# Output token sums behind the state updates, a head's squares as one step, operand loads of the output block behind P7

## The chip, the cores and the metric

The kernel runs on one core of one Trainium2 chip. The metric is device time in microseconds (us). Before the change, three runs took 1650.22, 1650.51 and 1651.77 us, so the median is 1650.51 us. One more execution was recorded by the hardware profiler. It took 1648.75 us by itself, and its instructions span 1647.0 us; TensorE ran at a mean granted clock of 0.998 of full speed.

## What is computed

Two layers act on one sequence of 512 tokens with 2048 features. In each layer:

- RMSNorm of the input, then one projection `z = h @ w_in` whose columns are split among a gated linear attention (4 heads: q, k of 128 columns, v of 256) and a softmax attention (8 heads of 128 columns), each with a SiLU gate of its own.
- Linear attention, in chunks of 64 tokens: `S_c = diag(a_c) S_{c-1} + sum_s k_dec_s v_s^T`, and each token reads the state of its own chunk, `o = q S_c`.
- Softmax attention: each token sees its own chunk of 64 and the eight before it (with 512 tokens: all earlier chunks), with a learned bias by clipped distance.
- Each head's output is RMS-normalised (`o * rsqrt(mean(o^2) + eps)`), scaled and multiplied by its SiLU gate. The two groups are concatenated, projected by `w_out`, normalised again and added to the layer's input.

Everything is in float32.

## The kernel before

**Products.** Float32 accuracy is made of two reduced parts: an operand is split into a high part (a cast on ScalarE, `split` at L108, or `high` at L203 for weights) and a low part (the difference, on VectorE, L109 and L207). Three matmuls, high x high, low x high and high x low, make one product. `std_gemm` (L323) multiplies in the plain way. `fast_gemm` (L399 and L409) multiplies two 512-column weight blocks at once by a scheme with seven sub-products (P1 to P7) instead of eight. For these, sums of token blocks (S1 to S4) and sums of weight blocks are needed. The token sums of a layer's input and of its output are formed by `make_sums` (L613 to L622: four adds on VectorE for each of four column blocks c; `put` then splits each result and stores it to DRAM, L607). Later a job loads them back into a ring of four buffers `sa` (L187).

**Jobs.** A `fast_gemm` is 28 jobs: (P1, c) for c = 0 to 3, four of P5, eight of P6 and P3 mixed, then four each of P7, P2 and P4. A job is 12 matmuls over 512 columns. Its weight load (`fetch`, L154) is traced up to five jobs ahead, its cast and its low part three to four ahead. In one layer the order is: the attention gates, the linear attention's gates, av, two attention query/key products (feature-major), the linear attention's key/query product (`PAIRS[4]`), its value product (`PAIRS[5]`), the output projection's first two blocks (plain), and the last two blocks as a `fast_gemm` with `end=True`.

**Work beside the products.** The attention heads and the linear attention are written as generators, put on a list `tasks`. After every job `pump` advances the first task by some steps (`rate`, 2.1 or 2 steps a job). `until` pumps at once until a condition holds. `delayed` runs a function after so many more steps. `attend` runs a pair of heads a and b by the list `ORDER`: S (scores of a 128-token tile, L847 to L857), T (transposes of its probabilities, L869 to L874), P (`mix`, L886: probabilities times values, into 128 columns of one PSUM bank `ps_o` a head, and a square sum of that tile on ScalarE, L892), G (`gate`: VectorE adds at L896, a power on GpSimd at L447, four multiplies at L900). Eight steps after G comes `turn`: transposes (L911), scaling (L914) and split, the store of the head's output for the output sums (L917, `fa`) and, for the second head of a pair, the store of the pair's two operand halves to DRAM (L923, `oa`). The pairs come in the order 2/3, 0/1, 6/7, 4/5.

**Loads of the operands.** `fetch_operands` runs after each job of the value product. Once (P1, 3) is past, it loads each pair's first half (L1176) into the buffer that P1's operand has left, as soon as the code has traced that pair's `turn`. The second halves are loaded at P4 (L1180).

**Linear attention.** For each of eight units (head h, half p): `outer` (L1048), `states` (L1067 and L1069, four chained updates on VectorE), `read` (L1082), `norm` (squares at L1092, L451, power on GpSimd), `gate` (L1100) and `turn` (L1110, L1121). `early_sums` forms the output sums of column blocks 2 and 3 beside the last four units, one of its steps for three of theirs. The sums of blocks 0 and 1 come after all units.

**What sets the order.** The code's order of tracing is a priority. A planner with a cost model of its own then puts each engine's instructions in order. Where an instruction isn't ready by that model, a later one goes first. On the chip each engine, and SyncE's and GpSimd's DMA queues too, works strictly through its planned order. `tc.issue_after(x)` adds that what is traced inside it stands behind x on x's engine. Buffers of one tag are shared: 8 of `t2` (most intermediate rows), 4 PSUM banks `mm` and 4 `ax`.

Of the kernel before, what the change touches and what calls it, by code (L numbers as in the profile page):

```python
# [15 lines left out]
P = 128  # L16
# [18 lines left out]
def hybrid_trunk(  # L35
# [107 lines left out]
    last_cast, last_load, last_low, last_norm = [None], [None], [None], [None]  # L143
    made = set()
    lows = []
    rows = {}
# [451 lines left out]
    def make_sums(l, end, tags, parts, chunks=range(4)):  # L598
        stage = [0]
        dst = (so_d if end else sa_d)[l]  # L600

        def put(name, c, src):
            op = slot(tags[stage[0] % 4], [2, 512], F32R)
            stage[0] += 1
            with tc.issue_after(last_cast[0]):
                split(op[:, 0, :], op[:, 1, :], src)
            nc.gpsimd.dma_start(dst[name, c], flat(op))  # L607
            made.add((l, end, name, c))

        for c in chunks:  # L610
            a11, a12, a21, a22 = parts(c)
            yield
            nc.vector.tensor_tensor(out=a22, in0=a21, in1=a22, op=ALU.subtract)  # L613
            put("S1", c, a22)
            yield
            nc.vector.tensor_tensor(out=a21, in0=a11, in1=a21, op=ALU.subtract)
            put("S3", c, a21)
            yield
            nc.vector.tensor_tensor(out=a22, in0=a22, in1=a11, op=ALU.subtract)
            put("S2", c, a22)  # L620
            yield
            nc.vector.tensor_tensor(out=a12, in0=a12, in1=a22, op=ALU.add)  # L622
            put("S4", c, a12)
            yield

# [57 lines left out]
    def layer(l):  # L683
# [150 lines left out]
        class Head:  # L834
# [41 lines left out]
            def mix(self, i):  # L876
                hd = self.hd
                if self.ps_o is None:
                    self.ps_o = aux()
                    self.sg = sgt([4, P])  # L880
                    nc.sync.dma_start(
                        self.sg, sg_d[l][1][:, hd * P : (hd + 1) * P].rearrange("(t p) c -> p t c", p=P)
                    )
                o = self.ps_o[:, i * P : (i + 1) * P]
                for j in range(i + 1):
                    nc.tensor.matmul(  # L886
                        o, self.pt[i][:, j * P : (j + 1) * P],
                        av[hd // 4, j // 2][:, j % 2, (hd % 4) * P : (hd % 4 + 1) * P],
                        start=(j == 0), stop=(j == i),
                    )  # L890
                jk = t2((P,), BF16)
                nc.scalar.activation(jk, o, AF.Square, scale=P ** -0.5, accum_out=self.ss[:, i : i + 1])  # L892

            def gate(self):
                v, cf = sm(4), sm(4)
# [9 lines left out]
            def turn(self):  # L905
                c, kk = self.hd // 2, self.hd % 2
                if kk == 0:
                    turned[c] = [slot(tag, [2, 512], F32R) for tag in ("g16", "g17")]
                ps = aux()
                for t in range(NT):  # L910
                    nc.tensor.transpose(ps[:, t * P : (t + 1) * P], self.sg[:, t, :], ident)  # L911
                kt = 8 + self.hd
                f = t2()
                nc.scalar.activation(  # L914
                    f, ps, AF.Copy, scale=gcol[:, l * 2 * KT + KT + kt : l * 2 * KT + KT + kt + 1]
                )
                nc.gpsimd.dma_start(of_att[l][c][:, kk, :], f)  # L917
                ks = slice(kk * 256, (kk + 1) * 256)
                for half in range(2):
                    z = turned[c][half]  # L920
                    split(z[:, 0, ks], z[:, 1, ks], f[:, half * 256 : (half + 1) * 256])
                    if kk:
                        nc.gpsimd.dma_start(oa_d[l][half, c], flat(z))  # L923

        ORDER = (
            "aS3 aS2 aS1 aS0 aT3 bS3 aT2 aP3 bS2 aT1 aP2 bS1 aT0 aP1 bS0 aP0 - aG "
            "bT3 bT2 bP3 bT1 bP2 bT0 bP1 bP0 - bG"
        ).split()

        def attend(hd, qk):  # L930
            heads = {"a": Head(hd, qk, 0), "b": Head(hd + 1, qk, 1)}

            def turn(h):
                h.turn()
                if h.hd % 2:
                    heads_done.add(hd)

            for _ in range(5 if hd == HEADS[0] else 0):
                yield
            for step in ORDER:  # L940
                if step == "-":
                    yield
                    continue
                h = heads[step[0]]
                if step[1] == "S":
                    h.scores(int(step[2]))
                elif step[1] == "T":
                    h.trans(int(step[2]))
                elif step[1] == "P":
                    h.mix(int(step[2]))  # L950
                else:
                    h.gate()
                    delayed.append([8, lambda h=h: turn(h)])
                yield
# [73 lines left out]
        class Unit:  # L1028
# [24 lines left out]
            def states(self):  # L1053
                h, p = self.h, self.p
                tag = "sg" if (2 * h + p) % 2 else "bias"
                self.sg = tmp.tile([P, 2, 256], F32, tag=tag, name=nm(tag), bufs=2)
                nc.sync.dma_start(
                    self.sg,
                    sg_d[l][0][p * 256 : (p + 1) * 256, h * 256 : (h + 1) * 256].rearrange("(t p) c -> p t c", p=P),
                )  # L1060
                prev = self.prev
                for q in range(4):
                    n = 4 * p + q
                    cur = self.st[:, q, :]
                    u = self.ps_u[q % 2][:, (q // 2) * 256 : (q // 2 + 1) * 256]
                    if prev is None:
                        nc.vector.tensor_copy(cur, u)  # L1067
                    else:
                        nc.vector.scalar_tensor_tensor(  # L1069
                            out=cur, in0=prev, scalar=a_end[:, h * 8 + n : h * 8 + n + 1], in1=u,  # L1070
                            op0=ALU.mult, op1=ALU.add,
                        )
                    prev = cur

            def read(self):
# [95 lines left out]
        def fetch_operands(k, c):  # L1171
            passed.add((k, c))
            for i in range(4):
                if ("P1", 3) in passed and 2 * i in heads_done and (0, i) not in op_att:
                    op_att[0, i] = slot(f"a11{i}", [2, 512], F32R)
                    nc.sync.dma_start(flat(op_att[0, i]), oa_d[l][0, i])  # L1176
# [193 lines left out]
```

## Time and profile before

| what | value |
|---|---|
| median of three runs | 1650.51 us (1650.22 to 1651.77) |
| profiled execution | 1648.75 us |
| its span, first to last instruction | 1647.0 us |
| TensorE matmul busy | 1626.9 us |
| VectorE busy | 1226.5 us |
| ScalarE busy | 904.6 us |
| GpSimd busy | 164.3 us |
| moved by DMA | 470.64 MB, mean 286 GB/s |

PE is TensorE's matmul, PEld its weight load, DVE VectorE, ACT ScalarE, POOL GpSimd, SP SyncE. In a timeline a row has the start and the length in us, the engine, the line of the kernel, the operation, the tile written and the tiles read, the shape and a count; in brackets the idle time before it and what ended it. A matmul record lasts longer than its turn on the engine, because matmuls are pipelined: their starts are about 0.23 us apart for 512 columns. A row of SPq or POOL with DMA_DIRECT2D is the issue of a transfer, not the transfer. In the table of waits a row names the waiting engine and line, then what it waited for, the total in us, the number of times and the longest.

### The profile page before, as it was taken

The numbers are of one execution on the slowest core, as the hardware profiler recorded it, in microseconds if no ns is written. First come the engines' busy times: TensorE is split into PE (matmuls) and PEld (weight loads), VectorE is DVE, ScalarE is ACT, GpSimd is POOL, SyncE is SP. The second block draws the span as 40 slices with busy tenths as digits, with TensorE's granted clock in tenths as the row PEclk, the third lists the DMA queues.
The fourth block names the chain that finished last, engine by engine and source line by source line (L and its number), as shares of the span: only waits on it lengthen the run. The fifth ranks groups of instructions, "written<-read, shape, count | busy, mean of one in ns | idle before, by whom it ended". The sixth has DMA issues, their size and how long they took to land.

```text
span 1647.0 us, 24886 instructions
## 1 busy us (share of the span) xinstructions
PE 1626.9 (99%) x9030; PEld 1393.8 (85%) x9030; DVE 1226.5 (74%) x1579; ACT 904.6 (55%) x1515; POOL 164.3 (10%) x261
## 2 busy tenths in 40 slices
PE   9999999999999999999999999999999999999997
PEld 7888889999988877688888888899999888776886
DVE  7567776877877875778877676768777768757887
ACT  7444544566666644454784445445657665445553
POOL 1210000000000101310132000000001001013101
PEclk9999999999999999999999999999999999999999
DMA  9978896858858796899879797868587678878996
GB/s 378 344 276 315 284 316 223 309 183 303 281 187 291 249 352 202 285 378 332 294 257 379 270 331 268 319 222 304 193 308 263 204 265 281 321 226 299 363 345 230
DMA packets 150778, 470.64 MB, mean 286 GB/s; under 512 B 16428, under 2 KB 35636, under 8 KB 150656
## 3 DMA queue, kind: packets, MB, share of 16 engines
q1 hardware_dynamic: 127632, 389.36, 68.4%
q0 software_dynamic: 22304, 78.41, 12.2%
q8 instruction: 71, 1.16, 0.3%
q10 hardware_dynamic: 720, 1.28, 0.2%
q14 instruction: 51, 0.42, 0.1%
HBM read 396.88 MB, written 72.11 MB: 285 GB/s over the span
## 4 chain that ended last, share of the span: by engine, by line
PE 98%; ACT 1%; DMA 1%; DVE 0%; issue 0%; DVEq 0%; POOL 0%; SPq 0%; ACTq 0%; POOLq 0%
PE mm L409 45%; PE mm L323 22%; PE mm L399 20%; PE ax L886 2%; PE ax L409 1%; PE ax L1048 1%; PE ax L869 1%; PE ax L1082 1%; PE ax L717 1%; PE ax L847 1%; PE ax L849 1%; PE ax L848 1%; DMA sa<-S 0%; PE ax L911 0%; PE ax L551 0%; PE ax L748 0%
## 5 line engine op out<-in xcount | busy, mean ns | idle before, releaser
L409 PE MATMUL mm<-wh,sa 128*128 128x512 f32 x1536 | 486.1, 391 | 2.4 <-DMA sa<-S 1.3
L203 ACT CAST wh<-raw 128x1024 fp32r<-128x1024 f32 x256 | 269.8, 1056 | 264.9 <-PE mm L409 110.8
L207 DVE TENSOR_TENSOR wl<-raw,wh 128x1024 fp32r<-128x1024 f32 x256 | 311.9, 1221 | 123.9 <-PE mm L409 38.7
L207 DVE TENSOR_TENSOR wl<-H,wh 128x1024 fp32r<-128x1024 f32 x224 | 273.0, 1221 | 112.5 <-PE mm L409 51.2
L203 ACT CAST wh<-H 128x1024 fp32r<-128x1024 f32 x224 | 235.2, 1052 | 213.9 <-PE mm L409 121.7
L409 PEld LDWEIGHTS mm<-wh,sa 128*128 128x128 f32 x1536 | 288.3, 188 | 63.9 <-ACT wh L203 3.2
L409 PE MATMUL mm<-wl,sa 128*128 128x512 f32 x768 | 300.1, 391 | 0.0
L399 PE MATMUL mm<-sa,wh 128*128 128x256 f32 x1280 | 238.0, 285 | 0.0
L399 PEld LDWEIGHTS mm<-sa,wh 128*128 128x128 f32 x1280 | 200.5, 191 | 0.4
L409 PE MATMUL mm<-wh,a 128*128 128x512 f32 x576 | 184.9, 391 | 0.0
L399 PE MATMUL mm<-sa,wl 128*128 128x256 f32 x640 | 181.1, 284 | 0.0
L323 PE MATMUL mm<-wh,a 128*128 128x512 f32 x512 | 169.0, 396 | 4.0 <-ACT a L108 1.2
L409 PEld LDWEIGHTS mm<-wl,sa 128*128 128x128 f32 x768 | 144.3, 188 | 29.9 <-issue 0.8
L197 DVE TENSOR_TENSOR H<-H,raw 128x1024 f32<-128x1024 f32 x120 | 145.7, 1219 | 2.3 <-DMA raw<-in_w_dram 0.7
L409 PEld LDWEIGHTS mm<-wh,a 128*128 128x128 f32 x576 | 108.0, 188 | 22.2
L399 PEld LDWEIGHTS mm<-sa,wl 128*128 128x128 f32 x640 | 122.3, 191 | 0.0
L323 PEld LDWEIGHTS mm<-wh,a 128*128 128x128 f32 x512 | 96.7, 189 | 27.7 <-DVE g L1228 2.0
L447 POOL TENSOR_TENSOR sm<-sm,mhalf 128x4 f32<-128x4 f32 (+2 forms) x40 | 51.9, 1299 | 677.5 <-DVE sm L896 448.6
L409 PE MATMUL mm<-wl,a 128*128 128x512 f32 x288 | 113.4, 394 | 0.0
L323 PE MATMUL mm<-wl,a 128*128 128x512 f32 x256 | 101.0, 395 | 0.0
L399 PE MATMUL mm<-a,wh 128*128 128x256 f32 x512 | 95.0, 284 | 0.0
L323 PE MATMUL mm<-wh,sa 128*128 128x512 f32 x256 | 87.0, 396 | 0.0
(206 smaller groups left out, 2327.8 us busy)
## 6 DMA issues: line engine op xcount, KB each, us to landing
raw<-in_w_dram SPq DMA_DIRECT2D x320, 512.0 KB, 5.5
sa<-S SPq DMA_DIRECT2D x192, 512.0 KB, 4.8
H<-in_w_dram SPq DMA_DIRECT2D x56, 512.0 KB, 4.4
sa<-A SPq DMA_DIRECT2D x48, 512.0 KB, 5.2
S<-g POOLq DMA_DIRECT2D x32, 512.0 KB, 7.6
oS<-g POOLq DMA_DIRECT2D x32, 512.0 KB, 6.5
sa<-oS SPq DMA_DIRECT2D x32, 512.0 KB, 6.0
sg<-t POOLq DMA_DIRECT2D x32, 256.0 KB, 5.8
```

The lines of the kernel that those rows point to most:

```text
L197: nc.vector.tensor_tensor(out=h, in0=h, in1=r, op=ALU.add)
L203: last_cast[0] = nc.scalar.copy(self.wh, src).ins
L207: last_low[0] = nc.vector.tensor_tensor(out=self.wl, in0=self.src, in1=self.wh.bitcast(F32), op=ALU.subtract).ins
L323: mm = nc.tensor.matmul(pss[o], a[:, part, t], rhs[:, kk, :], start=(i == 0 and kk == 0 and m == 0), stop=(i == n - 1 and kk == 1 and m == 2),
L399: nc.tensor.matmul(dst, lhs[:, kk, f], a[:, part, tok], start=(fresh and kk == 0 and m == 0 and ft % 2 == 0), stop=(c == c_last and kk == ...
L409: nc.tensor.matmul(out_ps[t], a[:, part, tok], rhs[:, kk, :], start=(fresh and kk == 0 and m == 0), stop=(c == c_last and kk == 1 and m == ...
L447: return nc.gpsimd.tensor_tensor(out=out_r, in0=v, in1=mhalf[:, : v.shape[-1]], op=ALU.pow).ins
L717: nc.tensor.matmul(ps[0:96, half * 256 : (half + 1) * 256], wga[kt // 10][:, kt % 10, :], op[:, i, (kt % 2) * 256 : (kt % 2 + 1) * 256], s ...
L847: nc.tensor.matmul(ps[:, :n], self.qh[:, t], self.kh[:, :n], start=True, stop=False)
L848: nc.tensor.matmul(ps[:, :n], self.qh[:, t], self.kl[:, :n], start=False, stop=False)
L849: nc.tensor.matmul(ps[:, :n], self.ql[:, t], self.kh[:, :n], start=False, stop=True)
L886: nc.tensor.matmul(o, self.pt[i][:, j * P : (j + 1) * P], av[hd // 4, j // 2][:, j % 2, (hd % 4) * P : (hd % 4 + 1) * P], start=(j == 0), ...
```

## The change

Three edits. First, in `make_sums` for the output sums, each of the four adds stands behind the state update that the code traced last. Second, the square sums leave `mix` and become a step Q of their own, behind the last mix of a head. Third, the loads of the four first operand halves are traced once (P7, 1) of the value product is past, and stand behind the latest load of weights or columns on SyncE; the last pair's first half is no longer stored to DRAM, and is copied from SBUF (`turned`) instead.

```diff
+        def add(out, in0, in1, op):
+            with tc.issue_after(last_state[0]) if end else nullcontext():
+                nc.vector.tensor_tensor(out=out, in0=in0, in1=in1, op=op)
...
-            nc.vector.tensor_tensor(out=a22, in0=a21, in1=a22, op=ALU.subtract)
+            add(a22, a21, a22, ALU.subtract)
...
-                jk = t2((P,), BF16)
-                nc.scalar.activation(jk, o, AF.Square, scale=P ** -0.5, accum_out=self.ss[:, i : i + 1])
+
+            def squares(self):
+                for i in range(NT):
+                    jk = t2((P,), BF16)
+                    nc.scalar.activation(
+                        jk, self.ps_o[:, i * P : (i + 1) * P], AF.Square, scale=P ** -0.5,
+                        accum_out=self.ss[:, i : i + 1],
+                    )
...
-                    if kk:
+                    if kk and (half or c != HEADS[-1] // 2):
                         nc.gpsimd.dma_start(oa_d[l][half, c], flat(z))
...
-            "aS3 aS2 aS1 aS0 aT3 bS3 aT2 aP3 bS2 aT1 aP2 bS1 aT0 aP1 bS0 aP0 - aG "
-            "bT3 bT2 bP3 bT1 bP2 bT0 bP1 bP0 - bG"
+            "aS3 aS2 aS1 aS0 aT3 bS3 aT2 aP3 bS2 aT1 aP2 bS1 aT0 aP1 bS0 aP0 aQ - aG "
+            "bT3 bT2 bP3 bT1 bP2 bT0 bP1 bP0 bQ - bG"
...
+                elif step[1] == "Q":
+                    h.squares()
...
-                        nc.vector.scalar_tensor_tensor(
+                        last_state[0] = nc.vector.scalar_tensor_tensor(
                             out=cur, in0=prev, scalar=a_end[:, h * 8 + n : h * 8 + n + 1], in1=u,
                             op0=ALU.mult, op1=ALU.add,
-                        )
+                        ).ins
...
-                if ("P1", 3) in passed and 2 * i in heads_done and (0, i) not in op_att:
+                if ("P7", 1) in passed and 2 * i in heads_done and (0, i) not in op_att:
                     op_att[0, i] = slot(f"a11{i}", [2, 512], F32R)
-                    nc.sync.dma_start(flat(op_att[0, i]), oa_d[l][0, i])
+                    src = flat(turned[i][0]) if i == HEADS[-1] // 2 else oa_d[l][0, i]
+                    with tc.issue_after(last_load[0]):
+                        nc.sync.dma_start(flat(op_att[0, i]), src)
```

The other three adds of `make_sums` change in the same way as the one shown.

More of the change, by code (lines that the diff above doesn't have):

```diff
@@ L142, in hybrid_trunk @@
     LEFT = {"P5": "S1", "P6": "S2", "P3": "S4", "P7": "S3", "P4": "A22"}
-    last_cast, last_load, last_low, last_norm = [None], [None], [None], [None]
+    last_cast, last_load, last_low, last_norm, last_state = [None], [None], [None], [None], [None]
     made = set()
@@ L612, in make_sums @@
             yield
-            nc.vector.tensor_tensor(out=a22, in0=a21, in1=a22, op=ALU.subtract)
+            add(a22, a21, a22, ALU.subtract)
             put("S1", c, a22)
             yield
-            nc.vector.tensor_tensor(out=a21, in0=a11, in1=a21, op=ALU.subtract)
+            add(a21, a11, a21, ALU.subtract)
             put("S3", c, a21)
             yield
-            nc.vector.tensor_tensor(out=a22, in0=a22, in1=a11, op=ALU.subtract)
+            add(a22, a22, a11, ALU.subtract)
             put("S2", c, a22)
             yield
-            nc.vector.tensor_tensor(out=a12, in0=a12, in1=a22, op=ALU.add)
+            add(a12, a12, a22, ALU.add)
             put("S4", c, a12)
```

## The prediction

> **What bounds the kernel now.** I read the page first, then what TensorE waited for, then the timelines around its longest waits. From the page:
>
> ```profile
> span 1647.0 us, 24886 instructions
> PE 1626.9 (99%) x9030; PEld 1393.8 (85%) x9030; DVE 1226.5 (74%) x1579; ACT 904.6 (55%) x1515; POOL 164.3 (10%) x261
> PE 98%; ACT 1%; DMA 1%; DVE 0%; issue 0%; DVEq 0%; POOL 0%; SPq 0%; ACTq 0%; POOLq 0%
> ```
>
> TensorE is busy 1626.9 of 1647.0 us and is 98% of the chain of waits. No edit here takes a matmul away, so only idle TensorE time can be won, 20.1 us in all. Its waits on others:
>
> ```profile
> PE ax L1110 <- issue: 2.2, 2, 1.1
> PE ax L886 <- ACT t L892: 1.8, 2, 0.9
> PE mm L409 <- DMA sa<-S: 1.3, 1, 1.3
> PE mm L323 <- ACT a L108: 1.2, 2, 0.6
> PE mm L323 <- DVE g L1228: 1.2, 2, 0.6
> PE mm L409 <- ACT wh L203: 1.2, 1, 1.2
> ```
>
> The columns are the total in us, the times and the longest. Those with count 2 come once in each layer. The two single ones are the same place in the two layers: the load of a token sum in layer 0, the cast of the weights that lands in its shadow in layer 1. So a layer has three sore places: mixes that wait for squares (0.9 us), a load in the value product (1.3 and 1.2), and the tail of the linear attention (1.1 + 0.6 + 0.6). Each edit of the diff touches one of them.
>
> **The squares as one step.** TensorE and ScalarE in layer 0, inside the key/query product:
>
> ```profile
> 520.62 0.60 PE L911 MATMUL ax<-cst,sg 128*128 128x128 f32 x4
> 521.06 1.06 PE L886 MATMUL ax<-g,t 128*128 128x128 f32 x8
> 523.01 0.71 PE L886 MATMUL ax<-g,t 128*128 128x128 f32 x4 [0.89 <-ACT t L892]
> 521.26 0.69 ACT L914 ACTIVATE t<-ax,gcol 128x512 f32<-128x512 f32 x1 [0.81 <-PE ax L911]
> 521.98 0.71 ACT L108 CAST g<-t 128x256 fp32r<-128x256 f32 x2
> 522.60 0.27 ACT L892 ACTIVATE t<-ax 128x128 bf16<-128x128 f32 x1
> ```
>
> The first mix (eight matmul records) ends at 522.12. The next mix of the same head writes other columns of the same PSUM bank, yet begins only at 523.01, after the square of the first. That square stood behind a scaling and two casts of another head. With the squares traced behind the last mix, no mix can wait for one: 0.89 us a layer, 1.78 us in two. The cost is not in the number of instructions, which is unchanged:
>
> ```profile
> L892 ACT ACTIVATE t<-ax x64: 257/277/312, 335.1 to 1380.3; 128x128 bf16<-128x128 f32 x64
> L892 ACT ACTIVATION_READ_ACCUMULATOR t<-ax x64: 191/194/237, 335.3 to 1380.4; 128x1 f32 x64
> ```
>
> A square and its accumulator read take at most 0.277 + 0.194 = 0.47 us. Three that ran between the mixes now stand behind the last, so the gate comes up to 3 x 0.47 = 1.41 us later. I price this at nothing. It is hidden by the turn of a head, traced eight pump steps behind its gate (almost four jobs of a product, 2.7 us each: 12 matmuls at 0.23 us, the step between the two L409 rows quoted last below). Without that cover it costs 1.41 us a layer, 2.8 in two. So this edit lies between -1.8 and +2.8. I take -1.8, because its row is a plain wait of exactly this kind.
>
> **The operand of the last head pair.** The value product of layer 0, as SyncE, GpSimd, the chain and TensorE show it:
>
> ```profile
> 576.17 1.07 POOL L923 DMA_DIRECT2D oa<-g  x2 [1.27 <-DVE g L109]
> 579.23 1.82 SPq L187 DMA_DIRECT2D sa<-S  x2
> 584.35 0.32 SPq L1176 DMA_DIRECT2D a<-oa  x1
> 579.23 7.24 DMA sa<-S
> 586.60 0.47 PE L409 MATMUL mm<-wh,sa 128*128 128x512 f32 x1 [1.28 <-DMA sa<-S]
> ```
>
> The pair's two operand halves are stored at 576.17 (512 KB each). SyncE stands still from 581.05 to 584.35 until the first of them has landed, because it wants to load it back. But the load that TensorE waited for went out ahead of that, at 579.23. What made it late is its own 7.24 us on the DMA engines, against this median:
>
> ```profile
> raw<-in_w_dram SPq DMA_DIRECT2D x320, 512.0 KB, 5.5
> sa<-S SPq DMA_DIRECT2D x192, 512.0 KB, 4.8
> 572.00:587.00 15.00, 13.72 (x62) 11.05 (x61) 9.50 (x10) 7.76 (x10) 1.66 (x3) 1.00 0.96 344
> 587.00:603.00 16.00, 16.00 (x78) 12.64 (x77) 12.61 (x15) 7.47 (x9) 0.00 (x0) 1.00 0.98 380
> ```
>
> In the last two rows, stretches of time, the DMA share (0.96) and the GB/s (344) stand at the end. The DMA engines are full while the pair is stored. The change drops one 512 KB store, 0.524 MB / 344 GB/s = 1.5 us of their time right ahead of the late load, and takes the load back out of this stretch. 1.5 us is more than the wait of 1.28. I take both waits away: 1.28 + 1.2 = 2.48 us. The other bound is 0, if the load is no earlier because the other half's store and 256 KB for the output sums still run beside it.
>
> The Trainium skill, "DMA: Bandwidth & Descriptors", section "Issuing engines are not separate DMA queues", says that copies started by any engine end up on the same 16 DMA engines and interleave. By it a store of GpSimd can delay a load of SyncE, as the 7.24 us beside 4.8 suggest; if queues were apart, this term would be 0 and the sum -1.78.
>
> **The four operand loads behind P7.** They were spread over the value product's first job groups. Now all four are traced behind P7's second job and behind the latest weight load, which by counting is that of P2's third job:
>
> ```profile
> 598.16 0.39 SPq L154 DMA_DIRECT2D raw<-in_w_dram  x1
> 601.40 1.70 SPq L154 DMA_DIRECT2D raw<-in_w_dram  x2
> 607.47 1.06 ACT L203 CAST wh<-raw 128x1024 fp32r<-128x1024 f32 x1 [1.21 <-PE mm L409]
> 610.38 1.40 DVE L367 SCALAR_TENSOR_TENSOR t<-mm,norm,ev 128x512 f32<-128x512 f32 x2
> 611.70 1.21 DVE L207 TENSOR_TENSOR wl<-raw,wh 128x1024 fp32r<-128x1024 f32 x1
> ```
>
> So 2.1 MB go out at about 598.6, where the DMA engines are 0.98 busy at 380 GB/s: 5.5 us of backlog. Next behind is the weight load at 601.40, landing by the median at 606.9, now 612.4. Its cast (1.06) and low part (1.21) end at 614.7. The read-out at 610.38 marks the end of P7; three jobs of P2, 2.7 us each, pass before TensorE wants this block, at about 618. Cover: 3 us, so I price it at nothing. The left sums of P4 are wanted later still. The copy from SBUF adds no wait for a store, and the buffers it reads (g16) are next wanted by the linear attention's turns some 40 us later. Without the cover each microsecond late is one in each layer.
>
> **The token sums.** VectorE and TensorE near the end of the linear attention:
>
> ```profile
> 665.43 0.69 DVE L613 TENSOR_TENSOR t<-t,t 128x512 f32<-128x512 f32 x1 [3.85 <-DMA t<-fg]
> 666.77 1.51 DVE L1069 SCALAR_TENSOR_TENSOR g<-g,a_end,ax 128x256 f32<-128x256 f32 x3
> 682.62 0.69 DVE L613 TENSOR_TENSOR t<-t,t 128x512 f32<-128x512 f32 x1 [1.15 <-DMA t<-fg]
> 683.22 0.48 DVE L1069 SCALAR_TENSOR_TENSOR g<-g,a_end,ax 128x256 f32<-128x256 f32 x1
> 671.40 1.08 PE L1082 MATMUL ax<-g,g 128*64 128x256 f32 x8
> 686.87 1.08 PE L1082 MATMUL ax<-g,g 128*64 128x256 f32 x8
> ```
>
> The adds wait for DMAs with state updates queued behind them. Tracing order puts the first add behind the fifth unit's states only, so its wait of 3.85 us stays in front of the sixth unit's. The add at 682.62 must now follow the last update, which comes about 1.15 + 0.6 us earlier. But the read of those states starts at 686.87 with no idle time before it, 3.2 us after they are made. TensorE takes it at its place among the projection's matmuls. So the edit moves a thing that nobody waits for: 0. The sums themselves are wanted in the next product, tens of us later. The bounds: the whole tail gone, 2 x (1.1 + 0.6 + 0.6) = -4.6, or each layer's two moved adds (0.69 each) pushed into the gate's way, 2 x 1.38 = +2.8. The value near 0 is nearest to the row without a wait.
>
> **The sum.** The profiled execution took 1648.75 us, its span and 1.75 around it. 1648.75 - 1.78 - 2.48 = 1644.5. The median of the runs, 1650.51, lies 1.76 above that execution, so I forecast 1646.3.
>
> **Rivals.** *Slower: two more pump steps for each head pair.* A pair's order has 28 steps, then 30, at 2.1 steps a job and 28 jobs a product (58.8). Counted through the code, heads 6 and 7 fall back: the last head's first transpose goes from after job 11 of the key/query product to after job 14, and the forced pumping ahead of its P3 read-out grows from 11 steps to 17. These rows matter there:
>
> ```profile
> 522.15 0.75 DVE L367 SCALAR_TENSOR_TENSOR t<-mm,norm,ev 128x512 f32<-128x512 f32 x1 [2.62 <-PE ax L886]
> 525.18 0.39 PE L409 MATMUL mm<-wh,a 128*128 128x512 f32 x1
> 525.41 0.40 PE L409 MATMUL mm<-wl,a 128*128 128x512 f32 x1
> ```
>
> The read-out of P3's second tile gets its buffer only when a mix has read its own; it ends at 522.90, and P2 can't write that bank before. TensorE returns to the product at 525.18, so 2.28 us are spare. Three jobs late is 8.2 us (36 matmuls); past 2.28 each one is idle time: 5.9 us a layer, 11.8 in two, giving 1658.1 in full. Mixes no longer held by squares take some of it back; with half of the slip, 1.8 a layer, the gains are nearly eaten (1649.9), and with two thirds, 3.2 a layer, it is 1652.7. It decides past a slip of 4.4 us, and ends slower past 6. For it: the product had no job of its own for TensorE between 520.6 and 525.2. Against it: mixes run sooner once no square holds them, and TensorE picks what is ready. Chance 0.22, around 1653.
>
> *Only one of the two waits goes:* the S load is late all the same, 1648.7, or a new wait replaces the squares', 1648.1. For it: the stretch is full of loads anyway. Chance 0.20.
>
> *The tail shortens too:* half of its 4.6 us, 1644.0. For it: ScalarE's in-order casts wait for those adds. Against: the unhurried read at 686.87. Chance 0.13.
>
> *The burst starves P2:* past the 3 us of cover; 2 us a layer would bring 1650.3. I count it with the second rival.
>
> **How the numbers follow.** The forecast has 0.45, and its own range is 1644.8 to 1648.3 (half of either term missing). No change means within 0.2%, 3.3 us, about what a measurement of this kernel can tell. Of the forecast's 0.45, 0.37 lies beyond that bound, 0.08 within; with the tail's 0.13 faster is 0.50; same is 0.08 + 0.20 = 0.28; slower 0.22. The range takes in the tail and two thirds of the slow case: 1641.5 to 1654.5; beyond it lie the slow case in full and the whole tail.
>
> **What would show it.** Right: no wait of L886 on L892; SyncE with no stop for a stored operand in the value product, a sum's load there under 6 us, no TensorE gap near 585 and 1403. Four loads in a row near 599 with the next weight load some 5 us longer in flight, and no TensorE gap at 618. The three gaps at the tail unchanged. Wrong: a gap before the key/query product's P2, with the read-out of L367 past 525; or a smaller span from gaps that I did not touch.

## The result and the profile after

The changed kernel takes 1642.78 us in the median of six runs (1642.08 to 1643.78), the kernel before 1650.42 us beside it (1649.57 to 1651.77): the ratio is 0.9955, with a 95% interval of 0.9945 to 0.9964. On the chip of the second set of experiments it was 0.9955 again (0.9942 to 0.9967). So the change wins 7.6 us; the forecast was 4.2. The profiled execution after took 1642.16 us.

The span and TensorE's share on the page of the changed kernel:

```profile
span 1640.4 us, 24886 instructions
PE 1623.6 (99%) x9030; PEld 1392.1 (85%) x9030; DVE 1227.6 (75%) x1579; ACT 905.5 (55%) x1515; POOL 178.2 (11%) x259
```

What TensorE waited for, of the changed kernel (total in us, times, longest). Its lines are shifted: L1110 of before is now L1122, L886 is L890, L1228 is L1242.

```profile
PE ax L1122 <- issue: 2.2, 2, 1.1
PE mm L323 <- ACT a L108: 1.2, 2, 0.6
PE mm L323 <- DVE g L1242: 1.2, 2, 0.6
```

The waits of mixes on squares are gone, and so are the two in the value product (the load in layer 0, the weight cast in layer 1). The three gaps at the linear attention's tail stand as they stood: 1.1, 0.6 and 0.6 us in each layer. TensorE's timeline around the former square wait, the read-out of P3's second tile on VectorE, and the issues of SyncE and GpSimd in the value product, all of the changed kernel:

```profile
519.89 1.72 PE L890 MATMUL ax<-g,t 128*128 128x128 f32 x14
521.45 1.04 PE L1006 MATMUL ax<-cst,t 128*128 128x128 f32 x8
522.24 0.48 PE L409 MATMUL mm<-wh,a 128*128 128x512 f32 x1
...
519.40 0.74 DVE L367 SCALAR_TENSOR_TENSOR t<-mm,norm,ev 128x512 f32<-128x512 f32 x1
...
574.23 0.54 POOL L933 DMA_DIRECT2D oa<-g  x1 [1.66 <-DVE g L109]
...
575.37 5.31 SPq L187 DMA_DIRECT2D sa<-S  x3
...
593.32 0.86 SPq L1190 DMA_DIRECT2D a<-oa  x2
594.24 0.54 SPq L1190 DMA_DIRECT2D a<-g  x1
594.88 0.53 SPq L1190 DMA_DIRECT2D a<-oa  x1
...
596.47 0.57 SPq L154 DMA_DIRECT2D raw<-in_w_dram  x1
```

The fourteen mix records run without a break, where before there were eight, 0.89 us of idle time and the rest. The read-out of P3 is done at 520.14 and no longer stands behind the mixes (522.90 before). One store of 512 KB is left at 574.23, SyncE has no stop for a stored operand, and the four operand loads go out in a row after 593. The weight load issued behind them at 596.47 lands at 606.35, 9.9 us later.

The whole gain can be laid out by place. The table takes the start of the same product matmul in two profiles: how much less (-) or more (+) time a kernel needed than the kernel before between two such points. The points lie at 6.4, 302.7, 582.4, 635.6 and 722.3 us of the profile before and at the same places of layer 1. "Key/query" reaches from late in the attention products to just ahead of the late load, "value" from there to the end of the value product, "tail" is the output projection's first block, in which the linear attention ends. "Total" runs from the first product matmul to the last. The stretches left out (the rest of the output projection, the start of layer 1 and the end) make up the difference to it; they come to 1.03 us at most in one place, in `join` to 2.83.

| profile | start | key/query 0, 1 | value 0, 1 | tail 0, 1 | total |
|---|---|---|---|---|---|
| after | -0.95 | -1.32, -1.31 | -1.53, -1.53 | -0.29, +0.15 | -6.53 |
| after_again | -0.95 | -1.31, -1.31 | -1.72, -1.42 | +0.12, -0.19 | -6.05 |
| squares | -0.92 | -1.33, -1.31 | +1.34, +0.69 | -0.04, +1.50 | +0.35 |
| loads | +0.43 | -0.03, 0.00 | -1.79, -1.64 | +0.96, +0.04 | -1.14 |
| sums | +0.04 | -0.01, 0.00 | 0.00, -0.27 | +0.01, +1.34 | +1.09 |
| loads_p7 | +0.55 | -0.01, 0.00 | +0.07, +0.17 | -0.06, +1.55 | +2.48 |
| sbuf | +0.64 | -0.01, 0.00 | -0.01, +0.04 | -0.04, +1.30 | +1.80 |
| no_sums | -0.99 | -1.32, -1.33 | -1.69, -1.29 | -0.07, +0.01 | -6.20 |
| no_loads | +0.17 | -1.31, -1.31 | +0.59, +1.32 | -0.27, +1.26 | +1.69 |
| no_squares | -0.96 | 0.00, +0.01 | -1.69, -1.59 | +0.52, -0.23 | -2.23 |
| steps | +0.10 | +1.71, +1.67 | -0.99, -1.95 | -0.02, +0.05 | +1.38 |
| split | +0.51 | -1.33, -1.31 | -0.18, -0.03 | +1.68, +1.76 | +1.36 |
| join | -0.96 | -1.31, -1.31 | -1.41, -1.67 | +9.03, +8.19 | +13.20 |

The columns "key/query" and "value" repeat wherever the same edits are in: the first to 0.03 us, the second to 0.4 in a layer with the load edits and to 0.8 without. The column "start" and the values between 0.5 and 1.6 us in "tail" do not go with any edit; the last section tells of them. Medians are the measure for a kernel, the table for a place.

### The profile page after: what moved, and what is told of

Same layout as the page of the kernel before. It is cut to its first block, busy times and chain, and to the rows that moved or that the text cites. A ratio compares the mean times of both kernels' runs of the same rounds, so it can differ in the third digit from the quotient of the medians.

```text
span 1640.4 us, 24886 instructions
## 1 busy us (share of the span) xinstructions
PE 1623.6 (99%) x9030; PEld 1392.1 (85%) x9030; DVE 1227.6 (75%) x1579; ACT 905.5 (55%) x1515; POOL 178.2 (11%) x259
## 3 DMA queue, kind: packets, MB, share of 16 engines
q10 hardware_dynamic: 720, 1.28, 0.2%
## 4 chain that ended last, share of the span: by engine, by line
PE 97%; DVE 1%; DMA 1%; ACT 1%; issue 0%; DVEq 0%; POOL 0%; SPq 0%; ACTq 0%; POOLq 0%
PE mm L409 45%; PE mm L323 21%; PE mm L399 20%; PE ax L890 2%; PE ax L409 1%; PE ax L873 1%; PE ax L1060 1%; PE ax L721 1%; PE ax L1094 1%; PE ax L853 1%; PE ax L852 1%; PE ax L851 1%; DMA t<-fg 0%; PE ax L921 0%; PE ax L551 0%
## 5 line engine op out<-in xcount | busy, mean ns | idle before, releaser
L447 POOL TENSOR_TENSOR sm<-sm,mhalf 128x4 f32<-128x4 f32 (+2 forms) x40 | 67.1, 1678 | 767.1 <-DVE sm L906 542.0
L409 PEld LDWEIGHTS mm<-wh,a 128*128 128x128 f32 x576 | 108.0, 188 | 22.5
```

Of the source, the lines that this page charges most:

```text
L409: nc.tensor.matmul(out_ps[t], a[:, part, tok], rhs[:, kk, :], start=(fresh and kk == 0 and m == 0), stop=(c == c_last and kk == 1 and m == ...
L447: return nc.gpsimd.tensor_tensor(out=out_r, in0=v, in1=mhalf[:, : v.shape[-1]], op=ALU.pow).ins
```

## The experiments

**Each edit alone.** First, only the squares and the step Q (the second edit of the diff):

```diff
+            def squares(self):
+                for i in range(NT):
...
-            "aS3 aS2 aS1 aS0 aT3 bS3 aT2 aP3 bS2 aT1 aP2 bS1 aT0 aP1 bS0 aP0 - aG "
+            "aS3 aS2 aS1 aS0 aT3 bS3 aT2 aP3 bS2 aT1 aP2 bS1 aT0 aP1 bS0 aP0 aQ - aG "
...
```

> The squares of a head as one step, nothing else changed. Own theory (the mix waited 0.89 us a layer for a square in the same bank): 1.8 to 2.1 us faster than before, no wait of a mix on a square, the gap of the value product's load (1.28 and 1.17) still there. Rival (the two added pump steps a pair delay the P3 read-out of the key/query product): slower by 2 us or more, with an idle TensorE before that product's P2. Rival (the parts help each other): under 1 us by itself.

Measured: 1649.91 us, ratio 0.9999 (0.9990 to 1.0008). The gain of 1.8 to 2.1 us did not come; by its number the second rival, that the parts help each other, is right. The wait on the squares is gone and the key/query column has its -1.33 and -1.31, but the value product gives it back, in layer 0 all of it (+1.34), in layer 1 half (+0.69). The waits of this kernel, the chain's row of the load that TensorE waited for, and the value product (TensorE, then SyncE's issues):

```profile
PE mm L409 <- DMA sa<-S: 2.4, 2, 1.6
...
575.28 9.10 DMA sa<-S
...
584.52 0.47 PE L409 MATMUL mm<-wh,sa 128*128 128x512 f32 x1 [1.56 <-DMA sa<-S]
625.38 0.97 PE L1056 MATMUL ax<-g,g 64*128 64x256 f32 x6
627.40 0.98 PE L1056 MATMUL ax<-g,g 64*128 64x256 f32 x6
...
575.28 2.59 SPq L187 DMA_DIRECT2D sa<-S  x2
582.18 0.32 SPq L1184 DMA_DIRECT2D a<-oa  x1
```

In layer 0 TensorE waits 1.56 us for the load in place of 1.28, in layer 1 0.83 in place of the 1.17 for the cast: 2.39 us in all, where it was 2.45. So it is not a longer wait that takes the gain: TensorE comes 2.4 us earlier than before (1.0 of it from the start), and the load lands 2.1 us earlier, at 584.38 instead of 586.47. What takes it is no wait at all: an outer product of the linear attention that ran in one piece of twelve (L1048 in before) now runs in two of six, and each takes as long as the twelve did, 0.9 us more in each layer. The run `split` below and the last section measure this.

Second, only the load edits: the store dropped, the loads behind P7, the copy from SBUF.

```diff
-                    if kk:
+                    if kk and (half or c != HEADS[-1] // 2):
...
-                if ("P1", 3) in passed and 2 * i in heads_done and (0, i) not in op_att:
+                if ("P7", 1) in passed and 2 * i in heads_done and (0, i) not in op_att:
...
+                    src = flat(turned[i][0]) if i == HEADS[-1] // 2 else oa_d[l][0, i]
+                    with tc.issue_after(last_load[0]):
...
```

> The four operand loads behind P7, the last pair's first half copied from SBUF and not stored; nothing else changed. Own theory (a store fewer frees the DMA engines, the load of the token sum lands in time): 2.5 us faster, and up to 3.8, since the same stage of the changed kernel is 1.9 us a layer shorter; gaps near 585 and 1403 gone, the wait of mixes on squares (0.9 a layer) still there. Rival (the burst starves P2): a gap some 20 us after the loads, and no gain. Rival (the parts help each other): under 1 us by itself.

Measured: 1647.89 us, ratio 0.9985 (0.9976 to 0.9994). The value product wins 1.79 and 1.64 us; the square waits (0.89 each) are still there.

Third, only the adds behind the state updates:

```diff
+            with tc.issue_after(last_state[0]) if end else nullcontext():
...
```

> Only the output token sums' adds stand behind the state updates. Own theory (the states' read does not wait for them): within 0.5 us of before, the tail's three gaps (1.1, 0.6, 0.6 a layer) unchanged. Rival (what the prediction missed, about 3 us, comes from here): 2 to 3 us faster, with shorter gaps or tighter reads at the tail.

Measured: 1649.98 us, ratio 0.9999 (0.9990 to 1.0007). The three medians stand 0.3, 2.3 and 0.3 us below the kernel before: 2.9 in all, while the whole change wins 7.6.

**Each edit left out.** So the parts don't add, and each was taken out of the changed kernel (the reverse of the diffs above); `after_again` is the changed kernel once more.

> Squares as one step and all of the load edits, the token sums' adds where they stood. If the parts simply add (squares alone ratio 0.9999, loads alone 0.9985), the ratio is 0.9984, some 2.6 us below the kernel before. If squares and loads help each other (the squares' gain of 1.2 us a layer was given back in the value product, where the stored operand's load still came late), both gains stay: 0.9975, 4 us, as the prediction's two terms have it, and the rest of the whole change's 0.9955 is the sums' part. If the sums' edit does nothing even beside the others, the ratio is that of the whole change, 0.9955. In the trace of the third case the tail's gaps are those of the whole change; in the second there is a gap of about 1.8 us at the last unit turn of the second layer, as squares alone and loads alone had it.

> Squares as one step and the adds behind the state updates; store and loads of the operand as before. If the parts add: 0.9998, within 0.4 us of the kernel before. If the sums' edit keeps the tail from the loss that squares alone showed there (a gap of 1.79 us instead of 1.09, and wider outer products): 0.9988 or so, 2 us. The load gaps of the value product (1.3 to 1.6 us) are there in either case.

> Load edits and the adds behind the state updates; each square stays behind its own mix. If the parts add: 0.9983, 2.7 us below before. If the sums' edit needs only one of the others beside it to save the tail: 0.9970, 5 us. The two waits of 0.89 us on a square are there in either case, so the whole change's 0.9955 is not reached.

> The changed kernel once more, beside the other three on their chip: 0.9955 if the surplus over the sum of the parts is the kernel's own, 0.9980 to 0.9985 if it lay in the chip or the session, as the sum of the parts alone (-0.3, -2.3 and -0.25 us) would have it.

Measured, all on one chip with the kernel before at 1650.54 us: `no_sums` 1643.89, ratio 0.9953 (0.9940 to 0.9965); `no_loads` 1650.25, 0.9995 (0.9986 to 1.0003); `no_squares` 1647.51, 0.9980 (0.9971 to 0.9989); `after_again` 1644.18, 0.9955 (0.9942 to 0.9967). Squares and load edits together are the whole change; the adds do nothing with either, and the theory that they protect the tail falls. The interaction is between the squares and the loads: the squares are worth nothing without the load edits (0.9995 beside the adds, 0.9999 alone), and some 4 us with them (0.9980 becomes 0.9955). The table shows where: the key/query product wins 1.3 us a layer in all kernels that have the squares. Only where the load edits are in does the value product let it through. The wait is not what differs:

```profile
PE mm L409 <- DMA sa<-S: 2.3, 2, 1.5
```

is the row of `no_loads`, where the kernel before had 1.3 and one more wait of 1.2 for a cast. The value product can be taken apart into the gap at the late load, the outer products, the reads of the states and its own matmuls (each from start to next start; layer 0, layer 1; more or less than the kernel before):

| profile | gap | outer products | reads | own matmuls |
|---|---|---|---|---|
| squares | +0.28, -0.33 | +0.90, +0.90 | 0, 0 | +0.16, +0.12 |
| no_loads | -0.48, +0.32 | +0.90, +0.90 | 0, 0 | +0.17, +0.10 |
| loads | -1.28, -1.17 | +0.11, +0.11 | -0.57, -0.57 | -0.04, -0.01 |
| after | -1.28, -1.17 | +0.11, +0.11 | -0.57, -0.57 | +0.22, +0.09 |
| loads_p7 | -0.06, +0.09 | +0.91, +0.91 | -0.57, -0.57 | -0.21, -0.27 |
| sbuf | 0.00, +0.08 | 0, 0 | 0, 0 | -0.01, -0.04 |
| steps | -0.44, -1.17 | 0.00, +0.01 | -0.57, -0.57 | +0.01, -0.22 |

With the squares alone TensorE comes earlier, the load comes earlier with it, and the gap stays on average as it was. The outer product in two pieces takes the gain back. With both load edits the planner leaves that unit in one piece. So the interaction, as far as the places show it, is the planner's order and not a wait; why it orders so is not shown. By the places it is worth 0.8 us a layer, by the medians 4.7 us in all (7.6 against 2.9). Each ratio is uncertain by 1.5 us or more, so its size stays open.

**The store or the place of the loads.** Two kernels divide the load edits. In `loads_p7` the loads stand behind P7, but all is stored and loaded as before:

```diff
-                if ("P1", 3) in passed and 2 * i in heads_done and (0, i) not in op_att:
+                if ("P7", 1) in passed and 2 * i in heads_done and (0, i) not in op_att:
...
+                    with tc.issue_after(last_load[0]):
...
```

> The four operand loads behind P7 and behind the latest load, but all four still come from DRAM and both halves of the last pair are still stored. Theory of the store (its 512 KB are what made the sum's load late): most of the gap of 1.28 and 1.17 us stays, 0 to 1 us faster than before. Rival (SyncE's stop for the stored operand, or the place of the three earlier loads, is what counts): as fast as with the copy from SBUF, 2.5 us or more.

In `sbuf` the store is dropped and the half is copied from SBUF, at the old place:

```diff
-                    if kk:
+                    if kk and (half or c != HEADS[-1] // 2):
...
-                    nc.sync.dma_start(flat(op_att[0, i]), oa_d[l][0, i])
+                    src = flat(turned[i][0]) if i == HEADS[-1] // 2 else oa_d[l][0, i]
+                    nc.sync.dma_start(flat(op_att[0, i]), src)
```

> The kernel before with the last pair's first operand half taken from SBUF and its 512 KB store dropped; the load stays at its old place, in the value product's first jobs, and the adds and squares are as before. If the store is what makes the load of the token sum late (the prediction's working), both gaps of 1.28 and 1.17 us in the value product are gone, the load is in flight for under 6 us, and the ratio is 0.9980 to 0.9985, as with all load edits but the squares. If the place behind P7 is what counts, the gaps stay and the ratio is 0.9995 to 1.0005. Loads behind P7 with the store kept gave 0.9999 and kept a gap of 1.3 us.

Measured: `loads_p7` 1650.67 us, ratio 0.9999 (0.9991 to 1.0008); `sbuf` 1651.09, 1.0004 (0.9995 to 1.0013). Neither half wins anything: the value columns are +0.07, +0.17 and -0.01, +0.04, and the gap stays in both (for `loads_p7` the small column also hides a read that got shorter and an outer product that got longer). The prediction's idea that the store alone is the cause misses. Nor is it SyncE's stop for the stored operand: `loads_p7` has no such stop and keeps the gap. GpSimd, SyncE and the wait in `loads_p7`:

```profile
576.62 1.06 POOL L923 DMA_DIRECT2D oa<-g  x2 [1.27 <-DVE g L109]
...
579.69 3.72 SPq L187 DMA_DIRECT2D sa<-S  x3
...
PE mm L409 <- ACT wh L203: 2.5, 2, 1.3
```

and GpSimd, SyncE and the wait in `sbuf`:

```profile
577.27 0.54 POOL L923 DMA_DIRECT2D oa<-g  x1 [1.61 <-DVE g L109]
...
576.71 0.54 SPq L1177 DMA_DIRECT2D a<-g  x1
580.00 3.72 SPq L187 DMA_DIRECT2D sa<-S  x3
...
PE mm L409 <- DMA sa<-S: 1.3, 1, 1.3
```

With the stores kept, two of 512 KB run in this stretch, and TensorE waits for a weight cast there, whose load went out at 576.01 beside them. With the store dropped, the reload no longer has to wait for it, goes out 3.3 us ahead of the load that TensorE needs (576.71 against 580.00) and takes the store's place: again two transfers of 512 KB, and the load at 580.00 takes 7.24 us from issue to landing, as it did before (7.17 in `loads_p7`). Only with both edits is there one. `loads`, which has just both, has no gap, and its load takes 5.80 us (580.33 to 586.13). That the number of large transfers is what counts is read from these four kernels; no run varies it by itself.

**The slower rival.** The kernel before with the two pump steps and no squares moved:

```diff
-            "aS3 aS2 aS1 aS0 aT3 bS3 aT2 aP3 bS2 aT1 aP2 bS1 aT0 aP1 bS0 aP0 - aG "
-            "bT3 bT2 bP3 bT1 bP2 bT0 bP1 bP0 - bG"
+            "aS3 aS2 aS1 aS0 aT3 bS3 aT2 aP3 bS2 aT1 aP2 bS1 aT0 aP1 bS0 aP0 - - aG "
+            "bT3 bT2 bP3 bT1 bP2 bT0 bP1 bP0 - - bG"
```

> The kernel before with two empty pump steps more for each head pair, at the places where the squares' steps stand after the change; no square is moved. By the prediction's slower rival the heads slip and the read-out of P3 in the key/query product comes late: with half of the slip 1.8 us a layer (ratio 1.002), with two thirds 3.2 (1.004), in full 5.9 (1.007), and a gap of TensorE ahead of P2 that was not there. If the slip is covered: 0.999 to 1.001, with the waits of 0.89 us on the squares in place or shifted.

Measured: 1651.37 us, ratio 1.0008 (0.9998 to 1.0017). The rival's mechanism is real. The read-out of P3 now ends at 524.84, and TensorE waits for it:

```profile
522.23 1.06 PE L886 MATMUL ax<-g,t 128*128 128x128 f32 x8
524.89 1.09 PE L994 MATMUL ax<-cst,t 128*128 128x128 f32 x8 [1.61 <-DVE t L367]
...
524.09 0.75 DVE L367 SCALAR_TENSOR_TENSOR t<-mm,norm,ev 128x512 f32<-128x512 f32 x1
```

It costs 1.71 and 1.67 us in the key/query product, near the half slip that the prediction gave as 1.8. But the value product returns 0.99 and 1.95 of it. The gap at the late load is 0.44 us shorter in layer 0 and gone in layer 1, as TensorE comes later to it; a read of the states in one piece instead of two gives 0.57 in each layer.

**What a split of the outer product costs.** The changed kernel, with a unit's matmuls traced half by half (`cc` is the half of 64 tokens, and of 64 rows of the array) instead of in turn:

```diff
-                for tt in range(2):
-                    ops = []
-                    for cc in range(2):
...
+                for cc in range(2):
+                    for tt in range(2):
...
```

> The changed kernel, but the outer product of a unit traces its 6 matmuls of one 64-row half ahead of the 6 of the other, in place of one of each in turn. The same 192 matmuls. If the halves of one unit run side by side when they alternate (12 in 0.90 us in one piece, 6 and 6 apart in 0.90 each), each unit in one piece now takes 1.8 us, and 12 to 14 of 16 units pay 0.9: 10 to 12 us more, about 1654. If a split costs because of the change between product and state matmuls, and not because of the halves, nothing changes: 1643.

Measured: 1650.45 us, ratio 0.9998 (0.9989 to 1.0007), some 7 us above the changed kernel. One unit of the changed kernel and the same unit of `split`, each with the next product matmul:

```profile
634.76 0.97 PE L1060 MATMUL ax<-g,g 64*128 64x256 f32 x12
635.67 0.50 PE L323 MATMUL mm<-wh,a 128*128 128x512 f32 x1
```

```profile
637.43 1.32 PE L1057 MATMUL ax<-g,g 64*128 64x256 f32 x12
638.68 0.50 PE L323 MATMUL mm<-wh,a 128*128 128x512 f32 x1
```

From its first matmul to the next product matmul the unit takes 0.91 us in turn and 1.25 half by half; in two pieces apart (the rows of `squares` above) 0.9 and 0.9. The expected direction is right, the size not: in one piece it costs 0.35 and not 0.9, since the two halves still overlap for a part of it (last section). Summed over 16 units the outer products take 22.5 us instead of 17.6 (from the starts of all 192 matmuls). Another 2 us of the loss are reads of the states, which come in two pieces more often (18.5 us instead of 16.2, idle time left out).

**Two pieces joined.** In the changed kernel one unit of each layer is still in two pieces of six, one half each (the first unit of a layer is in four, and stays so). `join` delays the successors in the second pair of heads, so that all twelve are planned together:

```diff
                 if k < 3:
+                    for _ in range(0 if j else (3, 1, 1)[k]):
+                        yield
                     new(k + 1)
```

> The changed kernel with three more pump steps ahead of a unit's successor, then one and one, in the second pair of heads alone. By the order of TensorE's instructions the one unit of a layer whose 12 outer products stood as 6 and 6 is then in one piece, and every read too. If a split costs 0.9 us as its rows say, 0.9 a layer is won: 1.8 us, ratio to before 0.9944 instead of 0.9955. If the later start of the units shows in the tail instead, no gain or a loss of up to the steps' 1.4 us a layer.

Measured: 1661.96 us, ratio 1.0071 (1.0058 to 1.0084), 19 us above the changed kernel. The pieces did join, and the outer products take 15.9 us instead of 17.6, the 0.9 a layer that was expected. But the tail loses 9.0 and 8.2 us, far more than the 1.4 of the rival:

```profile
PE ax L1122 <- DVE sg L1112: 8.3, 2, 4.5
PE mm L323 <- ACT a L108: 4.3, 2, 2.2
PE mm L323 <- ACT g L108: 4.3, 2, 2.2
...
685.99 0.48 PE L1122 MATMUL ax<-cst,sg 128*128 128x128 f32 x1 [4.54 <-DVE sg L1112]
686.40 1.98 PE L1094 MATMUL ax<-g,g 128*64 128x256 f32 x8
691.37 0.80 PE L323 MATMUL mm<-wh,g 128*128 128x512 f32 x1 [2.16 <-ACT g L108]
691.96 0.63 PE L323 MATMUL mm<-wl,g 128*128 128x512 f32 x1
```

The last units now end behind the projection's jobs, so their gates and casts stand bare: 7.2 and 6.3 us of the loss are idle time, and 1.5 in each layer are product matmuls at half clock behind it (last section). No version that beats the changed kernel came out of these runs.

## Why the prediction was right, and where its terms were off

The direction and the two places of the gain are right. The time is 3.5 us below the forecast and also below the forecast's own range (1644.8 to 1648.3). The whole range takes it in only because it was drawn down to 1641.5 for a tail that shortens, which did not come: that is luck. One premise is wrong, that "only idle TensorE time can be won": with the same 9030 matmuls TensorE's busy time fell from 1626.9 to 1623.6 us, as much as its idle time (20.1 to 16.8). Part of that is the clock at the start, part the pieces that the next points tell of. The terms, against the table:

- **Squares: -0.89 a layer expected, -1.32 measured.** The wait is gone, as said. The 320 mixes of L886 took 33.70 us before and 31.71 after, summed from start to start: 1.0 a layer, of which 0.89 is the wait. Of the other 0.3, 0.2 lies in the product's own matmuls and the rest in the attention's other work, whose order was planned anew. That the later squares cost nothing holds. (The 0.47 us for a square and its read are medians; the longest make 0.55. At a cost of nothing it makes no difference.) What the working left out is that the planner orders anew what comes later: in `squares` an outer product in two pieces takes back 0.9 a layer. So the sum of the terms holds in the changed kernel, and not for each edit alone.
- **The operand of the last pair: -1.24 a layer expected, -1.53 and -1.53 measured** (-1.79 and -1.64 in `loads`). The waits of 1.28 and 1.2 us went. The 1.5 us for a store is a good size where the reload leaves too: the same load takes 5.80 us in `loads` where it took 7.24 before, and 7.61 in the changed kernel (575.37 to 582.98) where it took 9.10 in `squares`. What the term missed is a read of the states. In the kernel before it ran in two pieces:

```profile
616.75 1.08 PE L1082 MATMUL ax<-g,g 128*64 128x256 f32 x6
617.75 0.50 PE L409 MATMUL mm<-wl,a 128*128 128x512 f32 x1
...
621.65 0.65 PE L1082 MATMUL ax<-g,g 128*64 128x256 f32 x2
622.23 0.50 PE L409 MATMUL mm<-wl,sa 128*128 128x512 f32 x1
```

Up to the next product matmul these take 1.00 and 0.58 us; all eight in one piece, as after, take 1.01. The step of the working that failed is "1.5 us is more than the wait": one store fewer does not free the load, as `sbuf` shows, since the reload takes its place. The half sentence beside it, that the reload leaves the stretch, was needed as much. The sign "under 6 us" holds in `loads` but not in the changed kernel, with its 7.61. There the load goes out earlier, as it does in `squares`, and lands only 0.13 us before its matmul starts at 583.11: there is no time to spare. The Trainium skill's rule in "DMA: Bandwidth & Descriptors", section "Issuing engines are not separate DMA queues", that copies of all engines interleave on the same DMA engines, agrees with `sbuf` and `loads_p7`: a store issued by GpSimd and a reload issued by SyncE delay the load alike.
- **The loads behind P7: 0, right.** In layer 0 weight loads behind them took 9.6 to 10.9 us instead of 5.6, and TensorE has no gap between 614 and 618. The cover of 3 us held.
- **The token sums: 0, right.** Alone 0.9999, left out 0.9953 beside 0.9955. The first add still waits 3.39 us with the sixth unit's updates behind it:

```profile
661.18 0.69 DVE L604 TENSOR_TENSOR t<-t,t 128x512 f32<-128x512 f32 x1 [3.39 <-DMA t<-fg]
661.78 1.51 DVE L1081 SCALAR_TENSOR_TENSOR g<-g,a_end,ax 128x256 f32<-128x256 f32 x3
```

- **The slower rival** was a fair one: its steps cost 1.7 us a layer where they stand alone. In the changed kernel, where no square holds the mixes, the read-out of P3 starts at 519.40, and the cost does not show. What in the new order brings that about was not taken apart. (The prediction's "TensorE picks what is ready" is, by the order described ahead of it, what the planner does.) Whether the squares without the two steps would win more was not tried.
- **The tail** keeps its three gaps, as the forecast had it; the rival in which it shortens falls. So does the one in which only one of the two waits goes.

The sum of the measured terms is 2 x 1.32 + 2 x 1.53 = 5.7 us, against 4.26 expected. The profiles differ by 6.6 us and the medians by 7.6. The 0.95 us at the start are part of the 6.6 and are not the change's (last section). So 1.9 us of the medians' 7.6 have no place in the profiles. A part of them goes with the clock: 81 later runs of the kernel before had a mean granted clock of 0.9973, where its profile had 0.998; the eleven runs of the changed kernel had 0.9980. Among the 81, those at 0.996 took 1651.4 us on average and those at 0.998 1649.6. Whether the change itself makes stretches of half clock rarer is not shown.

## What to carry to other kernels

A change in one place makes the planner order later work anew, and a microsecond won can be lost there. So lay the gain out by place, with waits and busy time apart, and try edits together as well as alone. When a transfer is taken out of a crowded stretch, ask which one moves up into the hole. And a busy engine can still lose time: count in how many pieces the same matmuls run, not only the gaps between them.

## What the runs showed of the hardware

**Halves side by side, and a price for each piece.** Twelve matmuls of 64 rows and 256 columns, the halves in turn, take 0.91 us, and six of one half alone take 0.90. The profile calls both busy. (The 0.90 are those of the two pieces in `squares`, up to the next product matmul.) The starts of the single matmuls show why: in the twelve they come in pairs, less than 0.01 us apart, and a pair every 0.12 us; in the six there is one every 0.12 us. Counted in such turns, pieces of 1, 2, 3, 5, 6, 8 and 9 turns take 0.31, 0.43, 0.55, 0.78, 0.90, 1.13 and 1.25 us: 0.12 a turn and 0.19 for the piece as such. The last is the unit of `split`, whose halves overlap in part. The Trainium skill, "TensorEngine Tiling (Array Packing)", section "Key Properties", says that different tiles of the array work in parallel and that a change of the tiling mode drains TensorE. The rows agree with the first. The 0.19 us of each piece are what the second would lead one to expect, but no run shows the drain itself.

**Half clock after short gaps.** In eight of fourteen profiles the first product matmuls, and in eight those behind the gaps at the tail (1.09 and 0.62 us, or one of 1.7 to 1.8, in `join` longer ones), run at half rate for two to three us. `sums`, then the kernel before, behind the same two gaps in layer 1; the last row of each is the stretch from 1511.8 to 1515.2 us, with TensorE's busy time and matmuls, the granted clock, the DMA share and GB/s:

```profile
1511.74 0.79 PE L323 MATMUL mm<-wh,a 128*128 128x512 f32 x1 [0.62 <-ACT a L108]
1512.34 0.63 PE L323 MATMUL mm<-wl,a 128*128 128x512 f32 x1
1512.76 0.63 PE L323 MATMUL mm<-wh,a 128*128 128x512 f32 x1
...
1511.80:1515.20 3.40, 3.40 (x8) 0.50 0.95 304
```

```profile
1512.09 0.50 PE L323 MATMUL mm<-wh,a 128*128 128x512 f32 x1 [0.62 <-ACT a L108]
1512.42 0.40 PE L323 MATMUL mm<-wl,a 128*128 128x512 f32 x1
1512.66 0.39 PE L323 MATMUL mm<-wh,a 128*128 128x512 f32 x1
...
1511.80:1515.20 3.40, 3.01 (x12) 1.00 0.98 330
```

Starts lie 0.43 us apart instead of 0.23, with equal gaps, and the granted clock is 0.50 instead of 1.00. The tail of most such rows of the table is 1.3 to 1.6 us longer for it (where the stretch begins later and runs into the third gap, 0.5 or 1.0), and the 0.95 us of the column "start" come from the same: the granted clock is full from 5.1 to 6.3 us on in the six profiles without it, and only from 9.8 us or later on in the eight with it, in four of them after a first stretch at full clock.

It goes with no edit that was tried: at the start `squares` has none and `no_loads`, which has the squares too, has it. What it goes with is where the gaps fall. In the record of the clock each half stretch at the tail lasts 3.4 us (in `join` three times that), and it begins on a grid of 3.4 us steps that each profile places differently. In the step ahead of it TensorE was busy for at most 0.56 of the time: 0.49 in `sums`, where both gaps lie in one step, against 0.61 in the kernel before, where the second gap reaches into the next. Steps at 0.52 and 0.53 went without, so the share alone does not decide it. The Trainium skill, "TensorE: Matmul & The Clock Gate", Part 1, describes a clock gate that halves TensorE's clock after an idle window of about 3.4 us, a window that runs freely, so that the same kernel meets it differently from run to run. The half clock, the length and the free grid agree; only the changed kernel was profiled twice here, so that one kernel meets it differently is not shown. The idle time does not agree: here 1.09 and 0.62 us with four transposes between them were enough. The same Part also tells of short idle times between groups of matmuls that make the clock swing, without a length for them; that is nearer.
